# A Jensen-Shannon divergence kernel: row groups in rotating buffers, new column ranges, and a last fold on ScalarE that takes the running sum as its bias

## The chip, the cores and the metric

The kernel runs on one core of a Trainium2 chip. A core has engines that work side by side, each with its own queue of instructions: TensorE (PE, matrix products, with its weight loads shown apart as PEld), VectorE (DVE), ScalarE (ACT), GpSimd (POOL) and SyncE (SP). They share an on-chip memory of 128 partitions (SBUF); TensorE writes to a second one (PSUM). Data comes from the outside memory by DMA, over 16 DMA engines. The metric is the device time of one execution in microseconds.

## The reference

Two inputs of 1,024 rows and 4,096 columns in float32, one float32 result for each row:

```python
m = 0.5 * (p + q)
kl_pm = np.sum(p * np.log(p / (m + 1e-8) + 1e-8), axis=-1)
kl_qm = np.sum(q * np.log(q / (m + 1e-8) + 1e-8), axis=-1)
return (0.5 * (kl_pm + kl_qm)).astype(np.float32)
```

The kernel takes the quotient apart: log p, log q and log m are taken on their own (each with the same scale inside the logarithm, SHIFT), and p(log p - log m) + q(log q - log m) is summed over the columns of a row.

## The kernel before, in words

The rows are dealt to the partitions so that each of 8 row groups (g = 0 to 7) holds 128 rows, one on each partition, with 4,096 columns of p and of q. Within a group the columns are cut into ranges. There are four cuts, each a list of widths for each group: LOADS (what one pair of transfers brings, L20), LOGS (what one logarithm of the data covers, L30), PRODUCTS (how wide a buffer of logarithms is, L40) and SUMS (what one sum p + q covers, L50). A number in what follows counts the ranges of its cut through all groups: q13 is the 14th range of LOGS.

The first two ranges (HW = 2) come in float32, p on SyncE's queue and q on ScalarE's (L171, L172). All others are cast to fp16 under way and are issued by GpSimd (L179, L180), p first, in the order of LOADS, with p and q of a range in the two halves of one tile. Each row group has a tile of its own, so nothing in the loads waits for a buffer.

The operations are named by a letter and a range:

- F (L257): TensorE adds p and q of a SUMS range by two matmuls with the identity into PSUM, 512 columns at a time. There are two PSUM tiles for this, used in turn. For the two float32 ranges VectorE adds them instead (a, L238).
- p and q (L274 to L294): ScalarE's logarithms of the data into a buffer `ab`. For the first SPLIT ranges p and q have an instruction each, later one instruction takes both, with twice the width.
- c (L296): ScalarE's logarithm of the sum, out of PSUM.
- u and x (L309, L318), groups 0 to 5: VectorE subtracts log m from both logarithms, then multiplies by p and q. The product goes over the data in place.
- m and s (L324, L337), groups 6 and 7 (APART = 6): VectorE multiplies p and q by their logarithms, and, apart from that, the sum by its logarithm, which needs no subtraction.
- X, M, S (L348): TensorE adds the columns of a product, 256 at a time, into an accumulator `acc` of the group, with half the identity as weights, or its negative for S.
- The last FUSED_M of the m and FUSED_S of the s are fused: VectorE multiplies and sums along the row in one instruction and keeps a running sum in a column of `run`, so that TensorE has nothing to add.
- f (L374): VectorE folds the 256 columns of `acc` to one number for each row, into a column of `res`. A, in group 7 only (L368): ScalarE does this with a Copy that accumulates; f7 then adds A's number to the running sum.
- W: matmuls whose result is not used.

The order on each engine is written out by hand in three texts: ACT_ORDER (L73), PE_ORDER (L78) and DVE_ORDER (L83). `after` (L405) says what each operation has to wait for: F for its PSUM tile, c for one of 4 buffers (C_BUFS), p and q for one of 5 buffers `ab` (AB_BUFS), products' additions for the accumulator, of which there are two. A loop (L439) emits from each text whatever has all its conditions emitted. Engines keep the order of their texts; the loads of GpSimd are emitted ahead of all that. The end of ScalarE's text is `c30 q29 c31 q30 q31 q32 A7`, of VectorE's `s31 m27 m28 m29 f7`. The result goes out by one DMA of SyncE (L470).

Of the kernel before, what the change touches and what calls it, by code (L numbers as in the profile page):

```python
# [13 lines left out]
AW = 256  # L14
AB_BUFS = 5
C_BUFS = 4

LOADS = [  # L20
    [512, 256, 832, 960, 768, 768],
    [512, 896, 832, 768, 1088],
    [1280, 1408, 1408],
    [1152, 1408, 1536],
    [1280, 1536, 1280],
    [1408, 1408, 1280],
    [256, 1536, 1536, 768],
    [2048, 2048],
]
LOGS = [  # L30
    [512, 256, 832, 960, 768, 768],
    [512, 896, 832, 768, 1088],
    [1280, 1408, 1408],
    [1152, 1408, 1536],
    [1280, 1536, 1280],
    [1408, 1408, 1280],
    [256, 1536, 1536, 768],
    [768, 1024, 896, 512, 512, 384],
]
PRODUCTS = [  # L40
    [512, 256, 832, 1728, 768],
    [512, 896, 832, 1856],
    [1280, 1408, 1408],
    [1152, 1408, 1536],
    [1280, 1536, 1280],
    [1408, 1408, 1280],
    [1792, 1536, 768],
    [768, 1024, 896, 512, 512, 384],
]
SUMS = [  # L50
    [512, 256, 448, 384, 384, 384, 960, 768],
    [512, 896, 832, 768, 1088],
    [1280, 1408, 1408],
    [1152, 1408, 1536],
    [1280, 1536, 1280],
    [1408, 1408, 1280],
    [256, 1536, 1280, 1024],
    [1536, 1408, 1152],
]
HW = 2  # L60
SPLIT = 5

APART = 6
FUSED_M = 1
FUSED_S = 4

# [2 lines left out]


ACT_ORDER = """  # L73
p0 q0 c0 p1 q1 c1 p2 q2 c2 c3 p3 q3 c4 c5 p4 q4 c6 q5 c7 q6 c8 q7 c9 q8 c10 q9 c11 q10 c12
q11 c13 q12 c14 q13 c15 q14 c16 q15 c17 q16 c18 c19 q17 q18 c20 c21 q19 c22 q20 c23 q21
c24 c25 q22 c26 q23 q24 c27 q25 c28 q26 c29 q27 q28 c30 q29 c31 q30 q31 q32 A7
"""
PE_ORDER = """  # L78
W22 F2 F3 X0 X1 F4 F5 X2 X3 F6 X4 X5 F7 F8 X6 F9 X7 F10 X8 F11 X9 F12 X10 X11 F13 W8 X12
F14 F15 X13 F16 X14 F17 X15 F18 X16 F19 X17 F20 X18 F21 X19 F22 X20 F23 X21 F24 F25 X22  # L80
F26 S25 X23 F27 F28 S26 X24 M21 F29 S27 M22 M23 F30 F31 M24 M25 W10 M26 W4 M27 M28
"""
DVE_ORDER = """  # L83
a0 a1 u0 x0 u1 x1 u2 u3 x2 x3 u4 u5 x4 x5 u6 x6 u7 x7 u8 x8 f0 u9 x9 u10 x10 u11 x11 u12
x12 u13 f1 x13 u14 x14 u15 x15 u16 x16 f2 u17 x17 u18 x18 u19 x19 f3 u20 x20 u21 x21 u22
f4 x22 u23 s25 x23 u24 s26 x24 m21 s27 f5 m22 s28 m23 s29 m24 f6 m25 s30 m26 s31 m27 m28
m29 f7
"""


# [1 line left out]
def kernel(  # L92
# [45 lines left out]
        return r[0] >= APART  # L138

    small = ctx.enter_context(tc.tile_pool(name="small", bufs=1))  # L140
    lnp = ctx.enter_context(tc.tile_pool(name="lnp", bufs=AB_BUFS))
    mid = ctx.enter_context(tc.tile_pool(name="mid", bufs=C_BUFS))
    psp = [
# [8 lines left out]
    for i in range(HW):  # L152
        t32 = small.tile([P, 2, loads[i][2]], fp32, tag=f"pq32_{i}")
        early.append(t32)
    data = []
    for g in range(n_rg):
        t16 = small.tile([P, 2, n_cols - (split if g == 0 else 0)], fp16, tag=f"pq{g}")
        data.append(t16)

    def pq(g, c0, w):  # L160
        if g == 0:
            for i in range(HW):
                if loads[i] == (g, c0, w):
                    return early[i]
            c0 -= split
            assert c0 >= 0
        return data[g][:, :, c0 : c0 + w]

    for i in range(HW):
# [3 lines left out]
    warm = small.tile([P, 1], fp32, tag="warm")  # L173
    nc.vector.memset(warm, 1.0)
    nc.scalar.activation(out=warm, in_=warm, func=Act.Ln)  # L175
    def cast_loads(some):
        for g, c0, w in some:
            v = pq(g, c0, w)
            nc.gpsimd.dma_start(out=v[:, 0, :], in_=pv[g, :, c0 : c0 + w])  # L179
            nc.gpsimd.dma_start(out=v[:, 1, :], in_=qv[g, :, c0 : c0 + w])  # L180

    cast_loads(loads[HW : HW + 1])
    ident = small.tile([P, P], fp16, tag="ident")
    make_identity(nc, ident)
    ones = small.tile([P, AW], fp16, tag="ones")
    nc.vector.memset(ones, 1.0)
    zero = small.tile([P, P], fp16, tag="zero")
    nc.vector.memset(zero, 0.0)
    cast_loads(loads[HW + 1 :])
    half = small.tile([P, P], fp16, tag="half")  # L190
    nc.vector.tensor_scalar(
        out=half, in0=ident, scalar1=0.5, scalar2=0.0, op0=Alu.mult, op1=Alu.add
# [22 lines left out]
    for g in range(n_rg):  # L215
        own = [o for o in dve_order if o == ("f", g) or (fused(*o) and range_of(*o)[0] == g)]
        if g < n_rg - 1 or act_folds:
            own = [o for o in own if o[0] != "f"] + [("f", g)]
        chain[g] = own

    ab, c, s, product, acc = {}, {}, {}, {}, {}
# [2 lines left out]
    def next_run(o, g):  # L224
        before = state["last"].get(g, 0.0)
        if o == chain[g][-1]:
            return before, res[:, g : g + 1]
        k = state["used"]
        state["used"] += 1
        state["last"][g] = run[:, k : k + 1]  # L230
        return before, run[:, k : k + 1]
# [92 lines left out]
    def op_m(k):  # L324
        g, c0, w = prods[k]
        u = pq(g, c0, w)
        if not fused("m", k):
            nc.vector.tensor_tensor(out=ab[k], in0=u, in1=ab[k], op=Alu.mult)  # L328
            product["M", k] = ab[k]
            return  # L330
        before, now = next_run(("m", k), g)
        nc.vector.tensor_tensor_reduce(
            out=ab[k], in0=u, in1=ab[k], scale=0.5, scalar=before,
            op0=Alu.mult, op1=Alu.add, accum_out=now,
        )

    def op_s(j):  # L337
        if not fused("s", j):
            nc.vector.tensor_tensor(out=c[j], in0=s[j], in1=c[j], op=Alu.mult)  # L339
            product["S", j] = c[j].unsqueeze(1)  # L340
            return
        before, now = next_run(("s", j), parts[j][0])
        nc.vector.tensor_tensor_reduce(  # L343
            out=c[j], in0=s[j], in1=c[j], scale=-0.5, scalar=before,
            op0=Alu.mult, op1=Alu.add, accum_out=now,
        )

    def add_up(kind, i):  # L348
# [9 lines left out]
        for n, (t, b) in enumerate(todo):  # L358
# [6 lines left out]
                stop=(kind, i) == adds[g][-1] and n == len(todo) - 1,  # L365
            )

    def op_A(g):  # L368
        folded = small.tile([P, 1], fp32, tag="folded")
        unused = small.tile([P, AW], fp16, tag="unused")  # L370
        nc.scalar.activation(out=unused, in_=acc[g][:, :AW], func=Act.Copy, accum_out=folded)  # L371
        state["folded"] = folded

    def op_f(g):  # L374
        if act_folds and g == n_rg - 1:
            nc.vector.tensor_tensor(  # L376
                out=res[:, g : g + 1], in0=state["folded"], in1=state["last"][g], op=Alu.add
            )
            return
        before, now = next_run(("f", g), g)  # L380
        if len(chain[g]) == 1:
            nc.vector.tensor_reduce(out=now, in_=acc[g][:, :AW], axis=AX, op=Alu.add)  # L382
# [22 lines left out]
    def after(kind, i):  # L405
# [19 lines left out]
        if kind == "W":  # L425
            return []
        if kind == "f":
            if act_folds and i == n_rg - 1:
                return chain[i][:-1] + [("A", i)]
            return chain[i][: chain[i].index(("f", i))] + adds[i]  # L430
        if kind == "A":
            return adds[i]
        return []

    accumulator(0)
    ops = dict(a=op_a, F=op_F, p=op_p, q=op_q, c=op_c, u=op_u, x=op_x, m=op_m, s=op_s, f=op_f, A=op_A)
    queues = [list(pe_order), list(act_order), list(dve_order)]
    emitted = set()
    while any(queues):  # L439
        moved = False  # L440
# [21 lines left out]
    want |= {(k.upper(), i) for k, i in want if k in "xms" and not fused(k, i)}  # L462
    want |= {("f", g) for g in range(n_rg)} | {("p", i) for i in range(SPLIT)}
    if act_folds:
        want.add(("A", n_rg - 1))
    assert emitted == want
    pe_order = [o for o in pe_order if o[0] != "W"]
    assert len(pe_order) + len(act_order) + len(dve_order) == len(want)

# [31 lines left out]
```

## Time and profile before

| | us |
|---|---|
| median of 4 runs (lowest to highest) | 97.81 (97.71 to 98.01) |
| profiled execution | 98.02 |
| its span, first to last instruction | 96.3 |
| ScalarE busy | 89.7 |
| VectorE busy | 81.7 |
| TensorE matmuls busy | 69.9 |
| ScalarE idle before logs of the data, in all | 1.6 |
| first logarithm of data starts, last one ends | 4.21, 92.50 |
| result in its tile | 93.90 |

The mean granted TensorE clock is 0.994. Lines of the profile name the engine, the line of the kernel, the operation, what is written and read, and the shapes (partitions x elements, type). In a timeline the first two columns are start and duration in us; what stands in brackets is how long the engine was idle just before and what ended that. Where neighbours of one kind are merged (x2), the shape is that of the first. In lines of groups the numbers after the bar are the busy time in us, the mean of one instruction in ns, and the idle time before them.

### The profile page before, as it was taken

What the parts mean: (1) busy time and instruction counts of PE and PEld (TensorE: products, weight loads), DVE (VectorE), ACT (ScalarE), POOL (GpSimd) and SP (SyncE); (2) the same over time, 40 slices, a digit from 0 to 9 for tenths busy, and PEclk for the clock granted to TensorE, in tenths of its full rate; (3) what the DMA queues carried; (4) which work ended last, traced back from release to release, by engine and by line L of the source; (5) the groups of instructions that cost most, each with busy time, mean ns of one, the idle gap of its engine ahead of it and who ended that gap; (6) DMA issues with size and microseconds to landing.
All of it is one profiled execution on the core that took longest, in us unless ns stands there. A gap on an engine that the chain in (4) does not pass through costs nothing.

```text
span 96.3 us, 1311 instructions
## 1 busy us (share of the span) xinstructions
PE 69.9 (73%) x468; PEld 44.7 (46%) x468; DVE 81.7 (85%) x87; ACT 89.7 (93%) x74; POOL 29.3 (30%) x60
## 2 busy tenths in 40 slices
PE   0797884976598568696785974984977979797740
PEld 0573441644456144462452642652652766566520
DVE  1279869999964988998979989979999999999990
ACT  3599999999979999999999999999999999999960
POOL 5974466443242424242332423336400000000000
PEclk9999999999999999999999999999999999999997
DMA  1999999999999999999999999999999999400000
GB/s 40 331 179 196 204 205 209 207 211 215 208 214 210 209 212 214 213 210 213 211 213 210 211 212 211 208 211 208 217 202 216 220 211 215 90 0 3 0 0 2
DMA packets 8503, 17.25 MB, mean 179 GB/s; under 512 B 1073, under 2 KB 3889, under 8 KB 8497
## 3 DMA queue, kind: packets, MB, share of 16 engines
q0 software_dynamic: 7776, 16.39, 89.9%
q1 hardware_dynamic: 432, 0.40, 1.4%
q10 hardware_dynamic: 288, 0.39, 1.2%
q8 instruction: 3, 0.05, 0.2%
q14 instruction: 4, 0.02, 0.1%
HBM read 33.55 MB, written 0.00 MB: 349 GB/s over the span
## 4 chain that ended last, share of the span: by engine, by line
ACT 48%; issue 22%; DVE 6%; PE 1%; ACTq 0%; DVEq 0%
ACT ab_t L281 30%; ACT c_t L299 18%; DVE t L321 2%; DVE c_t L343 1%; DVE ab_t L311 1%; PE acc_t L360 1%; DVE ab_t L328 1%; ACT unused L371 0%; ACTq L299 0%; DVE res L376 0%; ACTq L496 0%; ACTq L281 0%; DVEq L321 0%; DVE run L343 0%
## 5 line engine op out<-in xcount | busy, mean ns | idle before, releaser
L281 ACT ACTIVATE ab_t<-t 128x2816 f16<-128x2816 f16 (+15 forms) x38 | 62.6, 1685 | 1.6 <-DMA t<-in_p_dram 1.1
L265 PE MATMUL st<-t,ident 128*128 128x512 f16 (+4 forms) x144 | 34.0, 350 | 9.0 <-DMA t<-in_q_dram 7.9
L311 DVE TENSOR_TENSOR ab_t<-ab_t,c_t 128x2816 f16<-128x2816 f16 (+12 forms) x25 | 29.3, 1180 | 6.9 <-ACT c_t L299 6.1
L360 PEld LDWEIGHTS <-half 128*128 128x128 f16 x268 | 25.2, 97 | 20.1 <-issue 15.8
L299 ACT ACTIVATE c_t<-st 128x1408 f16<-128x1408 f32 (+13 forms) x30 | 32.3, 1099 | 0.0
L360 PE MATMUL acc_t<-t,half 128*128 128x256 f16 (+2 forms) x200 | 23.9, 264 | 8.2 <-DVE t L321 7.9
L321 DVE TENSOR_TENSOR t<-t,ab_t 128x2816 f16<-128x2816 f16 (+11 forms) x23 | 28.2, 1234 | 1.2
L265 PEld LDWEIGHTS <-ident 128*128 128x128 f16 x144 | 13.4, 97 | 23.1 <-issue 13.1
L179 POOL DMA_DIRECT2D t<-in_p_dram x27 | 14.5, 537 | 20.3 <-DMA t<-in_p_dram 19.3
L180 POOL DMA_DIRECT2D t<-in_q_dram x27 | 14.4, 532 | 19.7 <-DMA t<-in_q_dram 19.7
L360 PE MATMUL acc_t<-ab_t,half 128*128 128x256 f16 x68 | 8.9, 270 | 3.1 <-DVE ab_t L328 2.8
L328 DVE TENSOR_TENSOR ab_t<-t,ab_t 128x1536 f16<-128x1536 f16 (+5 forms) x8 | 9.3, 1171 | 0.1
L253 PE MATMUL acc_t<-ones,ident 128*128 128x256 f16 x22 | 4.2, 377 | 3.1 <-POOL ident masks.py:199 3.1
L253 PEld LDWEIGHTS <-ident 128*128 128x128 f16 x22 | 2.9, 136 | 4.1 <-POOL ident masks.py:199 3.1
L339 DVE TENSOR_TENSOR c_t<-st,c_t 128x256 f16<-128x256 f32 (+2 forms) x3 | 3.6, 1216 | 0.0
L343 DVE CUSTOM_DVE_ANT_0 c_t<-st,c_t,run 128x1408 f16<-128x1408 f32 (+1 forms) x2 | 3.1, 1546 | 0.0
L343 DVE CUSTOM_DVE_ANT_0 c_t<-st,c_t 128x1024 f16<-128x1024 f32 (+1 forms) x2 | 3.0, 1484 | 0.0
L253 PE MATMUL acc_t<-ones,zero 128*128 128x256 f16 x22 | 2.9, 273 | 0.0
L175 ACT ACT_TABLE_LOAD x1 | 1.3, 1283 | 1.7 <-PEq L485 1.7
L382 DVE TENSOR_REDUCE res<-acc_t 128x1 f32<-128x256 f32 x6 | 2.5, 417 | 0.0
L253 PEld LDWEIGHTS <-zero 128*128 128x128 f16 x22 | 2.1, 98 | 0.2
L321 DVE TENSOR_TENSOR ab_t<-t,ab_t 128x1024 f16<-128x1024 f32 (+1 forms) x2 | 1.9, 958 | 0.1
(24 smaller groups left out, 9.7 us busy)
## 6 DMA issues: line engine op xcount, KB each, us to landing
t<-in_p_dram POOLq DMA_DIRECT2D x5, 352.0 KB, 12.6
t<-in_q_dram POOLq DMA_DIRECT2D x5, 352.0 KB, 13.0
t<-in_p_dram POOLq DMA_DIRECT2D x4, 384.0 KB, 11.8
t<-in_q_dram POOLq DMA_DIRECT2D x4, 384.0 KB, 12.0
t<-in_p_dram POOLq DMA_DIRECT2D x4, 320.0 KB, 13.1
t<-in_q_dram POOLq DMA_DIRECT2D x4, 320.0 KB, 12.8
t<-in_p_dram POOLq DMA_DIRECT2D x2, 512.0 KB, 13.1
t<-in_q_dram POOLq DMA_DIRECT2D x2, 512.0 KB, 14.4
```

What stands on the lines that cost most here:

```text
L179: nc.gpsimd.dma_start(out=v[:, 0, :], in_=pv[g, :, c0 : c0 + w])
L180: nc.gpsimd.dma_start(out=v[:, 1, :], in_=qv[g, :, c0 : c0 + w])
L253: nc.tensor.matmul(out=acc[g][:, :AW], lhsT=weights, rhs=ones, start=alone, stop=alone)
L265: nc.tensor.matmul(out=st[:, b : b + m], lhsT=ident, rhs=v[:, t, b : b + m], start=t == 0, stop=t == 1,)
L281: nc.scalar.activation(out=ab[k][:, which, o : o + w], in_=pq(g, c0, w)[:, which, :], func=Act.Ln, bias=TINY, scale=SHIFT,)
L299: nc.scalar.activation(out=c_t[:, :w], in_=s[j], func=Act.Ln, bias=SHIFT * 1e-8, scale=SHIFT * 0.5)
L311: nc.vector.tensor_tensor(out=v, in0=v, in1=c[j].unsqueeze(1).to_broadcast([P, 2, parts[j][2]]), op=Alu.subtract,)
L321: nc.vector.tensor_tensor(out=into, in0=u, in1=v, op=Alu.mult)
L328: nc.vector.tensor_tensor(out=ab[k], in0=u, in1=ab[k], op=Alu.mult)
L339: nc.vector.tensor_tensor(out=c[j], in0=s[j], in1=c[j], op=Alu.mult)
L343: nc.vector.tensor_tensor_reduce(out=c[j], in0=s[j], in1=c[j], scale=-0.5, scalar=before, op0=Alu.mult, op1=Alu.add, accum_out=now,)
L360: nc.tensor.matmul(out=acc[g][:, :m], lhsT=less if kind == "S" else half, rhs=v[:, t, b : b + m], start=(kind, i) == adds[g][0] and n == 0 ...
```

## The change

Row groups no longer have a tile each: six tiles (DATA_BUFS) rotate, so that groups 6 and 7 take those of groups 0 and 1. A load is an operation L of its own with an order of its own; a load of group g waits until all products of group g - 6 have been added by TensorE.

All four cuts have new widths. The number of ranges: LOADS 29 before and 28 after, LOGS 33 and 28, PRODUCTS 30 and 24, SUMS 32 and 31. The widest buffer of logarithms grows from 1,856 to 2,816 columns; in groups 3 and 4 one logarithm of data covers 2,048 columns and so two loads. In groups 0 and 1 the first 7 ranges have p and q apart (SPLIT 5 to 7). The last group's logarithms end in ranges of 256, 256 and 128 columns, where they ended in 512, 512 and 384. The fused sums are the last five (FUSED_S 4 to 5), so that one of group 6 is among them. The three orders are new.

In group 7 there is no f any more. A is an Identity of ScalarE with the running sum as its bias, which adds it to each of the 256 columns before they are accumulated; so that it counts once, the fused operations of group 7 scale their sums by 1/256. A writes the result's column itself. f6 comes last on VectorE.

```diff
+DATA_BUFS = 6
 LOADS = [
-    [512, 256, 832, 960, 768, 768],
-    [512, 896, 832, 768, 1088],
-    [1280, 1408, 1408],
+    [352, 608, 864, 1088, 1184],
+    [1280, 1536, 1280],
     [1152, 1408, 1536],
-    [1280, 1536, 1280],
-    [1408, 1408, 1280],
-    [256, 1536, 1536, 768],
+    [1024, 1024, 1024, 1024],
+    [1024, 1024, 1024, 1024],
+    [1664, 1152, 1280],
+    [1920, 896, 640, 640],
     [2048, 2048],
 ]
 LOGS = [
...
+    [352, 608, 864, 1088, 1184],
+    [1280, 1536, 1280],
     [1152, 1408, 1536],
-    [1280, 1536, 1280],
+    [2048, 2048],
+    [2048, 2048],
     [1408, 1408, 1280],
-    [256, 1536, 1536, 768],
-    [768, 1024, 896, 512, 512, 384],
+    [1280, 1280, 1536],
+    [1152, 1024, 768, 512, 256, 256, 128],
 ]
 PRODUCTS = [
...
+    [352, 608, 864, 2272],
+    [1280, 2816],
+    [2560, 1536],
+    [2048, 2048],
+    [2048, 2048],
+    [1408, 2688],
+    [1280, 1280, 1536],
+    [1152, 1024, 768, 512, 256, 256, 128],
 ]
 SUMS = [
...
+    [352, 608, 512, 352, 896, 736, 640],
+    [1280, 1536, 1280],
     [1152, 1408, 1536],
-    [1280, 1536, 1280],
+    [1024, 1024, 1024, 1024],
+    [1024, 1024, 1024, 1024],
     [1408, 1408, 1280],
-    [256, 1536, 1280, 1024],
-    [1536, 1408, 1152],
+    [1280, 1280, 1536],
+    [1536, 1408, 640, 512],
 ]
-SPLIT = 5
+SPLIT = 7
-FUSED_S = 4
+FUSED_S = 5
 ACT_ORDER = """
...
+p0 q0 c0 p1 q1 c1 p2 q2 c2 c3 p3 q3 c4 p4 q4 c5 c6 p5 q5 c7 p6 q6 c8 q7 c9 q8 c10 q9 c11
+q10 c12 c13 q11 c14 c15 q12 c16 c17 q13 c18 c19 q14 c20 q15 c21 c22 q16 c23 q17 c24 q18
+c25 q19 c26 q20 c27 q21 c28 q22 c29 q23 c30 q24 q25 q26 q27 A7
 """
 PE_ORDER = """
...
+W22 F2 F3 X1 X0 F4 X2 X3 F5 F6 X4 F7 X5 X6 F8 X7 F9 F10 X8 F11 X9 X10 F12 F13 X11 F14 W8
+F15 X12 F16 X13 F17 X14 F18 X15 F19 X16 F20 X17 X18 F21 F22 X19 X20 F23 X21 F24 X22 F25
+S24 F26 X23 M14 F27 M15 S25 W6 F28 M16 F29 M17 F30 W4 M18 W4 M19 W3 M20 M21 M22
 """
 DVE_ORDER = """
...
+a0 u0 a1 x0 u1 x1 u2 u3 x2 x3 u4 x4 u5 u6 x5 x6 u7 f0 x7 u8 x8 u9 x9 u10 x10 f1 u11 x11
+u12 x12 u13 u14 x13 x14 f2 u15 u16 x15 x16 u17 u18 x17 x18 f3 u19 u20 x19 x20 u21 f4 x21
+u22 x22 u23 s24 x23 m14 s25 m15 s26 f5 m16 s27 m17 s28 m18 s29 m19 s30 m20 m21 m22 m23 f6
 """
...
+    datap = ctx.enter_context(tc.tile_pool(name="datap", bufs=DATA_BUFS))
...
-    cast_loads(loads[HW : HW + 1])
+    def op_L(i):
+        g, c0, w = loads[i]
+        if g not in data:
+            t16 = datap.tile([P, 2, n_cols], fp16, tag="pq")
+            data[g] = t16
+        v = pq(g, c0, w)
+        nc.gpsimd.dma_start(out=v[:, 0, :], in_=pv[g, :, c0 : c0 + w])
+        nc.gpsimd.dma_start(out=v[:, 1, :], in_=qv[g, :, c0 : c0 + w])
+    op_L(HW)
...
-            out=ab[k], in0=u, in1=ab[k], scale=0.5, scalar=before,
+            out=ab[k], in0=u, in1=ab[k], scale=0.5 * share(g), scalar=before,
...
-            out=c[j], in0=s[j], in1=c[j], scale=-0.5, scalar=before,
+            out=c[j], in0=s[j], in1=c[j], scale=-0.5 * share(g), scalar=before,
...
+    def share(g):
+        return 1.0 / AW if act_folds and g == n_rg - 1 else 1.0
     def op_A(g):
-        folded = small.tile([P, 1], fp32, tag="folded")
         unused = small.tile([P, AW], fp16, tag="unused")
-        nc.scalar.activation(out=unused, in_=acc[g][:, :AW], func=Act.Copy, accum_out=folded)
-        state["folded"] = folded
+        before, now = next_run(("A", g), g)
+        nc.scalar.activation(
+            out=unused, in_=acc[g][:, :AW], func=Act.Identity, bias=before, accum_out=now
+        )
     def op_f(g):
-        if act_folds and g == n_rg - 1:
-            nc.vector.tensor_tensor(
-                out=res[:, g : g + 1], in0=state["folded"], in1=state["last"][g], op=Alu.add
-            )
-            return
...
         if kind == "A":
-            return adds[i]
+            return chain[i][:-1] + adds[i]
+        if kind == "L":
+            g = loads[i][0] - DATA_BUFS
+            return adds[g] if g >= 0 else []
         return []
...
+    load_order = [("L", i) for i in range(HW + 1, len(loads))]
+    queues = [load_order, list(pe_order), list(act_order), list(dve_order)]
```

## The prediction

> **What bounds the kernel now.** I read the page's busy shares first, then ScalarE's timeline, then GpSimd's (it issues the casting loads), then the last stretch of all engines. The time is made against the profiled execution: 98.02 us, span 96.3 us, so 1.72 us lie around the span; the median of the runs is 97.81, 0.21 lower. A change in the span is taken over to the median as it stands.
>
> From the page:
> ```profile
> PE 69.9 (73%) x468; PEld 44.7 (46%) x468; DVE 81.7 (85%) x87; ACT 89.7 (93%) x74; POOL 29.3 (30%) x60
> DMA  1999999999999999999999999999999999400000
> ```
> ScalarE and the DMA engines both have no room: the transfers are dense until slice 34 (about 82.9 us), ScalarE to the end. From ScalarE's timeline:
> ```profile
> 24.19 2.08 ACT L281 ACTIVATE ab_t<-t 128x2176 f16<-128x2176 f16 x1
> 26.10 1.14 ACT L299 ACTIVATE c_t<-st 128x1088 f16<-128x1088 f32 x1
> 27.77 2.34 ACT L281 ACTIVATE ab_t<-t 128x2560 f16<-128x2560 f16 x1 [0.53 <-DMA t<-in_q_dram]
> 30.02 1.22 ACT L299 ACTIVATE c_t<-st 128x1280 f16<-128x1280 f32 x1
> 31.14 2.55 ACT L281 ACTIVATE ab_t<-t 128x2816 f16<-128x2816 f16 x1
> ...
> 34.82 2.54 ACT L281 ACTIVATE ab_t<-t 128x2816 f16<-128x2816 f16 x1
> 37.26 1.33 ACT L299 ACTIVATE c_t<-st 128x1408 f16<-128x1408 f32 x1
> 38.49 2.12 ACT L281 ACTIVATE ab_t<-t 128x2304 f16<-128x2304 f16 x1
> ```
> and from GpSimd's:
> ```profile
> 22.86 0.53 POOL L179 DMA_DIRECT2D t<-in_p_dram  x1 [0.78 <-DMA t<-in_p_dram]
> 24.16 0.53 POOL L180 DMA_DIRECT2D t<-in_q_dram  x1 [0.77 <-DMA t<-in_q_dram]
> 26.38 0.53 POOL L179 DMA_DIRECT2D t<-in_p_dram  x1 [1.70 <-DMA t<-in_p_dram]
> 27.97 0.53 POOL L180 DMA_DIRECT2D t<-in_q_dram  x1 [1.06 <-DMA t<-in_q_dram]
> 29.64 0.53 POOL L179 DMA_DIRECT2D t<-in_p_dram  x1 [1.14 <-DMA t<-in_p_dram]
> 31.34 0.53 POOL L180 DMA_DIRECT2D t<-in_q_dram  x1 [1.18 <-DMA t<-in_q_dram]
> ```
> Eight casting transfers go out without a wait at the start; after that each issue waits for a landing. So I take issue n+8 as the sign that transfer n landed, about 0.23 us earlier (the matmul that waited for q started at 9.99, GpSimd's issue stands at 10.23). Transfer 20, the first q of row group 2, so landed at 27.74, and ScalarE started its log at 27.77: it ran hand to mouth. The next landed at 31.11; its log began at 31.14. The one at 34.55 (issue 34.79) was used at 34.82. After that ScalarE is late by itself and never waits. The law: q of a range lands at 7.6 us (the matmul wait at 7.62) plus 512 bytes (one column of one input, 128 rows of 4 bytes) at 420 GB/s (twice the 210 written, since the cast halves the bytes), 1.219 ns, for each column of p and of q after the first 3,200. It puts the end of group 1 at 23.67 (23.93 seen) and the end of group 2 at 33.66 (34.55 seen). The 0.65 us more came in one jump, at the 1.70 us wait, while the page's GB/s row there reads 208 to 214: one lane was late, not the whole flow.
>
> **What the Trainium skill says.** "DMA: Bandwidth & Descriptors", section "Why a DMA increments its semaphore by 16 and not by 1": a transfer counts as landed only when each of its engines has reported, so one late engine holds it. The trace agrees with the jump at full rate, but shows no single engine. "ScalarE: Activation LUTs", "What ACT_TABLE_LOAD costs": 0.833 ns an element, and about 93 ns for each pointer operand. The step from 31.14 to 33.60 for 2,816 elements is 2.46 us, 0.11 over the elements; and the same 256 elements from PSUM take 463 ns with a bias and 383 without:
> ```profile
> L299 ACT ACTIVATE c_t<-st 128x256 f16<-128x256 f32 x1 | 0.5, 463 | 0.0
> L371 ACT ACTIVATE unused<-acc_t 128x256 f16<-128x256 f32 x1 | 0.4, 383 | 0.7 <-PE acc_t L360 0.7
> ```
> The same page, "Table sets: the hidden batching unit": identity and copy sit in every set as filler, so Identity in place of Copy should load no table. No run here shows Identity.
>
> **Part by part.**
> *ScalarE's sum.* Steps in the trace: a log of SBUF data costs its elements at 0.8333 ns plus 0.095 us (2.44 for 2,816 at 34.82), a log of the sums in PSUM plus 0.052 (1.23 for 1,408 at 37.26). Before: from 34.82, 65,664 elements, 20 and 17 instructions: 54.72+1.90+0.88 = 57.50, that is 92.32; the last log ends at 92.50, so 0.18 for an end. The change keeps 98,304 elements and has 66 instructions for 70 (35 logs of loads for 38, 31 of sums for 32): 0.34 us less in all. But that is worth only what the landings let through. In the new order, latest landing plus remaining work plus 0.18:
> - q2 (1,824 columns in): lands 8.2, 83.16 left: 91.5. q4: 13.7+77.64+0.18 = 91.5. q7: 23.9+67.78+0.18 = 91.9.
> - q9 (10,752 columns): 30.8+61.41+0.18 = 92.4.
> - q10 (end of group 2): 34.55 as before, 66,048 elements, 18 and 19 instructions left = 57.74: 92.47.
> - q11, now 2,048 columns, needs two loads of 1,024, 14,336 columns in. Between the landings 37.33 and 40.78 (issues 37.56 and 41.01) of 13,440 and 14,848 columns that is 39.5; 52.85 left: 92.53.
> - q12: 44.45+47.53+0.18 = 92.2; later ones less.
> So ScalarE ends its last log at about E = 92.5, as before: a first load of 352 columns may start it near 3.9 instead of 4.21 (160 columns of both inputs, 0.39 us), and it waits that off again. From start to end without waits it would be 3.9+86.94+0.18 = 91.0, the lower bound.
>
> *The loads' buffers.* A load of group 6 waits for the products of group 0 to be added, which the fold of group 0 at 19.83 shows done; GpSimd gets to transfer 41 at about 49.6 by the old issues. Group 7 waits for group 1 (fold at 32.68), issues near 60. Queued behind such a wait is every later load, but the margin is over 25 us: cost 0. That wait is absent from the old trace; a satisfied one costs at most some tens of ns on a queue that waits 39 us for landings anyway.
>
> *Sums just in time.* c24 needs 1,920 columns landed: 64.5 (end of group 5, issue 64.74) plus 3,840 x 1.219 = 69.2, plus six matmuls, 1.1 us (1.02 for five seen): 70.3, where ScalarE wants it at 92.5-0.18-21.79 = 70.5. c27: 79.4+1.6 = 81.0 against 81.2. c28: 83.0+1.2 = 84.2 against 84.5. All hold, by 0.2 to 0.3; if a wide load lands 0.5 later they cost 0.3.
>
> *VectorE.* 24 pairs of subtraction and product for 25, one product more in groups 6 and 7; the elements are the same except 192 more columns in fp32 at the start, 0.2 us in the addition and 0.2 in the product, hidden by its 6.9 us of waiting before subtractions. In the end it must follow ScalarE. An operation takes its elements at 0.96 GHz (two at once in fp16) plus 0.075 between starts (3,584: 1.94 us). From the end of c28: s28 ends at 1.57, m18 (log ready at 1.80) 2.97, s29 3.71, m19 4.67, s30 5.28, m20 5.89, m21 6.23, m22 6.60, while ScalarE's last log ends at 6.54. It follows with 0.06 lost. Fusing one sum more changes a product into one of the same rate and spares PE its adds.
>
> *The end.* Now:
> ```profile
> 92.53 1.02 DVE L332 CUSTOM_DVE_ANT_0 ab_t<-t,ab_t,run 128x768 f16<-128x768 f16 x1
> 93.23 0.38 ACT L371 ACTIVATE unused<-acc_t 128x256 f16<-128x256 f32 x1 [0.73 <-PE acc_t L360]
> 93.48 0.08 DVE L332 DVE_READ_ACCUMULATOR2_ANT run<- 128x1 f32 x1
> 93.51 0.19 ACT L371 ACTIVATION_READ_ACCUMULATOR unused<-acc_t 128x1 f32 x1
> 93.74 0.16 DVE L376 TENSOR_TENSOR res<-folded,run 128x1 f32<-128x1 f32 x1 [0.18 <-ACT unused L371]
> ```
> From the last log's end (92.50) to the result (93.90) 1.40 us. New: m23 has 256 elements, 1,017-512/0.96 = 484 ns; with its read it ends at E+0.06+0.50 = E+0.56. A7 now waits for it: 0.04 handover (93.70 to 93.74 the other way), 0.47 from its start to the end of its read (93.23 to 93.70) and 0.08 for the bias: E+1.15. M22 is two matmuls behind m22, done at about E+0.45, so not last. f6 beside it: 0.47+0.08 after m23, earlier than A7. The addition, 0.16 and its handover, is gone. Gain 0.25 (0.15 if the handover doubles, 0.31 if VectorE loses nothing). The output's transfer stays as it is.
>
> Sum: E unchanged (92.50 to 92.53), the end 0.25 shorter: 97.81-0.25 = 97.56; with E at q10's 92.47, 97.5. I take 97.5.
>
> **Rivals.**
> 1. *The late lane does not come back* (other widths, other moments). Then group 2 ends near 33.7, q10 gives 91.6 and c24 comes in time too: 0.85 us less, with the end 1.1: 96.7. For it: the delay was one jump. Against: all later landings keep 0.8 to 1.0 behind the law, and the new loads of group 1 are as wide as those at which it came. Chance 0.22.
> 2. *Slower: q11 waits for its second load.* A further delay like the first, 0.65 us, before the end of its two loads: 40.15+52.85+0.18 = 93.2, result 94.3, 0.45 later: 98.3. It decides from a landing at 39.7 (E of 92.75). For it: this log has no slack and needs four transfers in place of two. Against: only one such jump in 54 transfers. Chance 0.14.
> 3. *Identity brings a table load*, 1.28 us as the one at the start, 0.5 of it beside m23: 98.4. Chance 0.04.
> 4. *The end gains nothing*, because VectorE lags or the read-accumulator hand-over is longer: 97.8. Chance 0.1.
>
> **How the numbers follow.** The first forecast has 0.5. A difference of 0.2% (0.2 us) is about what a measurement can tell from none. Forecast: 0.36 of its half clearly faster, 0.12 within, 0.02 slower; rival 1 faster; rivals 2 and 3 slower; rival 4 within: faster 0.36+0.22 = 0.58, same 0.12+0.10 = 0.22, slower 0.02+0.14+0.04 = 0.20. The range takes rival 1 and reaches to where rival 2 begins to cost: 96.6 to 98.2; the forecast's own is 97.2 to 97.8.
>
> **What would show it.** ScalarE's logs of groups 0 to 3 should start within 0.1 us of landings, and after q11 none should wait; its last log should end at 92.3 to 92.7. The result should stand 1.1 to 1.2 us after it, with A7 near 0.46 us and no second table load. A last log before 92 means the lane was not late; a wait before q11, c24 or c27 means that these bind.

## The result, and the profile after

The changed kernel takes 97.76 us (median of 36 runs), the kernel before, run beside it, 97.94 us (55 runs): ratio 0.9982, 95% interval 0.997 to 0.9995, so 0.05 to 0.29 us less. That is faster, but by less than was predicted: 97.5 was 0.31 below the 97.81 it started from; what was measured is 0.18. The span of the profiled execution fell from 96.3 to 96.0 us. Ratios here and below leave out executions more than 1.5% above the fastest of their kernel; medians count all.

ScalarE's timeline of the changed kernel, at the place where the loads used to bind and at the end:

```profile
28.66 1.11 ACT L300 ACTIVATE c_t<-st 128x1152 f16<-128x1152 f32 x1
30.08 2.55 ACT L282 ACTIVATE ab_t<-t 128x2816 f16<-128x2816 f16 x1 [0.31 <-DMA t<-in_q_dram]
32.54 1.32 ACT L300 ACTIVATE c_t<-st 128x1408 f16<-128x1408 f32 x1
33.76 2.75 ACT L282 ACTIVATE ab_t<-t 128x3072 f16<-128x3072 f16 x1
...
81.82 2.23 ACT L282 ACTIVATE ab_t<-t 128x2304 f16<-128x2304 f16 x1
84.55 1.34 ACT L300 ACTIVATE c_t<-st 128x1408 f16<-128x1408 f32 x1 [0.50 <-PE st L266]
85.79 1.90 ACT L282 ACTIVATE ab_t<-t 128x2048 f16<-128x2048 f16 x1
...
90.02 2.40 ACT L282 ACTIVATE ab_t<-t 128x1024 f16<-128x1024 f16 x4
93.09 0.47 ACT L377 ACTIVATE unused<-acc_t,run 128x256 f16<-128x256 f32 x1 [0.66 <-PE acc_t L362]
93.46 0.19 ACT L377 ACTIVATION_READ_ACCUMULATOR unused<-acc_t,run 128x1 f32 x1
```

The log at 30.08 is q9, still hand to mouth with its load; q10, at 33.76, follows its predecessor without a wait, 0.8 us before the moment at which the prediction let its data land. So ScalarE was early. Then, at 84.55, c28 waits 0.50 us for its sum on TensorE, a wait that the kernel before does not have. The last log ends at 92.42 (90.02+2.40), before at 92.50. The result stands at 93.65, before at 93.90.

What c28 waited for is in TensorE's timeline of the same kernel:

```profile
81.61 0.82 PE L254 MATMUL acc_t<-ones,zero 128*128 128x256 f16 x6
82.27 0.81 PE L266 MATMUL st<-t,ident 128*128 128x512 f16 x3
83.81 0.70 PE L266 MATMUL st<-t,ident 128*128 128x512 f16 x3 [0.74 <-DMA t<-in_q_dram]
```

F28 has six matmuls. It did three, then stood until q of the last load landed, at about 83.8, and ended at 84.51. The sum covers columns 1,536 to 2,944 of group 7; the last load brings columns 2,048 to 4,096. F28 needs 896 of its 2,048 columns and waits for all of them.

To see where the landings went, I read GpSimd's issues as the prediction did and took off the prediction's law. Positive is late; each number is for q of the last range that ends at or before the column count:

| columns of each input | before | changed |
|---|---|---|
| end of the second casting load (2,560; 2,912) | +0.06 | -0.56 |
| 8,192 | +0.26 | -0.55 |
| 9,472; 9,344 | +0.95 | +0.13 |
| 12,288 | +0.90 | +0.06 |
| 20,480 | +0.98 | +0.39 |
| 26,368; 26,496 | +0.92 | +0.27 |

The changed kernel starts 0.6 us ahead, and meets a jump at the same place (0.68 against 0.69 us; that the two sizes agree is chance, they run from 0.28 to 1.04 in the twelve traces of this document).

### The profile page after: what moved, and what is told of

Its sections match the earlier page's. It is cut to its first block, busy times and chain, and to the rows that moved or that the text cites. A ratio compares the mean times of both kernels' runs of the same rounds, so it can differ in the third digit from the quotient of the medians.

```text
span 96.0 us, 1291 instructions
## 1 busy us (share of the span) xinstructions
PE 69.4 (72%) x461; PEld 44.6 (46%) x461; DVE 80.9 (84%) x86; ACT 89.8 (94%) x70; POOL 28.3 (29%) x58
## 4 chain that ended last, share of the span: by engine, by line
DMA 81%; issue 7%; DVE 3%; ACT 3%; POOL 2%; PE 1%; DVEq 0%; ACTq 0%; POOLq 0%
DMA t<-in_p_dram 68%; DMA t<-in_q_dram 13%; ACT ab_t L282 2%; DVE c_t L345 2%; DVE ab_t L329 1%; POOL t L180 1%; PE st L266 1%; POOL t L181 1%; ACT unused L377 0%; DVEq L500 0%; POOL ident masks.py:199 0%; POOL ident masks.py:197 0%; ACTq L500 0%; ACT c_t L300 0%; POOLq L500 0%
## 5 line engine op out<-in xcount | busy, mean ns | idle before, releaser
L282 ACT ACTIVATE ab_t<-t 128x2560 f16<-128x2560 f16 (+15 forms) x35 | 61.2, 1782 | 1.0 <-DMA t<-in_p_dram 0.7
L312 DVE TENSOR_TENSOR ab_t<-ab_t,c_t 128x2048 f16<-128x2048 f16 (+10 forms) x24 | 28.9, 1223 | 8.1 <-ACT c_t L300 5.4
L300 ACT ACTIVATE c_t<-st 128x1024 f16<-128x1024 f32 (+9 forms) x29 | 31.1, 1101 | 0.5 <-PE st L266 0.5
L362 PE MATMUL acc_t<-t,half 128*128 128x256 f16 (+1 forms) x192 | 23.5, 268 | 9.2 <-DVE t L322 9.0
L322 DVE TENSOR_TENSOR t<-t,ab_t 128x2048 f16<-128x2048 f16 (+9 forms) x22 | 27.5, 1272 | 0.5
L362 PE MATMUL acc_t<-ab_t,half 128*128 128x256 f16 (+2 forms) x74 | 9.0, 267 | 1.3 <-DVE ab_t L322 0.7
L329 DVE TENSOR_TENSOR ab_t<-t,ab_t 128x2560 f16<-128x2560 f16 (+6 forms) x9 | 9.6, 1088 | 0.3 <-ACT ab_t L282 0.2
L345 DVE CUSTOM_DVE_ANT_0 c_t<-st,c_t,run 128x1408 f16<-128x1408 f32 (+2 forms) x3 | 3.3, 1102 | 0.5 <-ACT c_t L300 0.5
L345 DVE CUSTOM_DVE_ANT_0 c_t<-st,c_t 128x1536 f16<-128x1536 f32 x2 | 3.5, 1752 | 0.0
L340 DVE TENSOR_TENSOR c_t<-st,c_t 128x1280 f16<-128x1280 f32 x2 | 3.0, 1486 | 0.0
```

Of the source, the lines that this page charges most:

```text
L282: nc.scalar.activation(out=ab[k][:, which, o : o + w], in_=pq(g, c0, w)[:, which, :], func=Act.Ln, bias=TINY, scale=SHIFT,)
L300: nc.scalar.activation(out=c_t[:, :w], in_=s[j], func=Act.Ln, bias=SHIFT * 1e-8, scale=SHIFT * 0.5)
L312: nc.vector.tensor_tensor(out=v, in0=v, in1=c[j].unsqueeze(1).to_broadcast([P, 2, parts[j][2]]), op=Alu.subtract,)
L322: nc.vector.tensor_tensor(out=into, in0=u, in1=v, op=Alu.mult)
L345: nc.vector.tensor_tensor_reduce(out=c[j], in0=s[j], in1=c[j], scale=-0.5 * share(g), scalar=before, op0=Alu.mult, op1=Alu.add, accum_out=now,
L362: nc.tensor.matmul(out=acc[g][:, :m], lhsT=less if kind == "S" else half, rhs=v[:, t, b : b + m], start=(kind, i) == adds[g][0] and n == 0 ...
```

## The experiments

Every ratio is to the kernel before, run beside it on the same chip. The changed kernel's own is 0.9982 (0.997 to 0.9995).

**The last load, cut in two.** The theory: c28 pays for the last load's width. One line:

```diff
     [1920, 896, 640, 640],
-    [2048, 2048],
+    [2048, 896, 1152],
 ]
 LOGS = [
```

> The changed kernel with the last load of group 7 (2,048 columns) cut into 896 and 1,152; all logs, sums and orders as they are. Theory (the last transfer holds c28): c28 waited 0.50 us in the changed kernel because its sum reaches into the last 2,048 columns, whose q landed at about 83.8; with the cut those columns are there some 2.8 us earlier, the wait goes, the last log ends near 91.9 instead of 92.42, and the time falls by 0.4 to 0.5 us (ratio to before about 0.994). Rival (TensorE's order or its PSUM tile holds the sum): no wait goes, ratio 0.998 as now. Second rival (two transfers more land later in all): slower than now, 0.999 to 1.002.

Measured: 97.17 us, ratio 0.9878 (0.9842 to 0.9914). TensorE and ScalarE, in the timelines of this kernel:

```profile
82.36 1.35 PE L266 MATMUL st<-t,ident 128*128 128x512 f16 x6
```

```profile
81.63 2.23 ACT L282 ACTIVATE ab_t<-t 128x2304 f16<-128x2304 f16 x1
83.75 1.34 ACT L300 ACTIVATE c_t<-st 128x1408 f16<-128x1408 f32 x1
...
89.22 2.40 ACT L282 ACTIVATE ab_t<-t 128x1024 f16<-128x1024 f16 x4
```

F28 runs through its six matmuls at once, c28 follows q21 without a wait, and the last log ends at 91.62. The wait was the transfer's: TensorE's order and its PSUM tile are as they were. In this trace the landings were also about 0.2 us earlier than in the changed kernel's, so its 0.8 us is more than the 0.5 of the wait. The ratio is below the 0.994 expected, and it rests on six executions, so I ran it again:

> last_load_cut once more on this chip, for the next one to be compared with, and since it rests on few executions. Theory: c28 does not wait, last log near 91.7; 0.5 to 0.8 us faster than the changed kernel, ratio to before 0.990 to 0.994. Rival (its 0.988 was a matter of that chip's runs of before): 0.996 to 0.998.

Measured: 97.21 us, ratio 0.9905 (0.9873 to 0.9936), again clear of the changed kernel's interval. This version beats both kernels, the changed one by 0.8 to 1.0%. In its trace, too, c28 has no wait, though its landings after the jump were about 0.4 us later than the changed kernel's (+0.53 at 9,344 columns); so its last log ends at 92.22 and not near the 91.7 expected. The two ratios make the gain over the changed kernel 0.75 to 1.0 us. The wait that went accounts for 0.26 to 0.50 (the size of c28's wait in two traces with the uncut load); where the rest comes from is not shown.

The same cut in the kernel before is the control, since nothing waits there:

```diff
     [256, 1536, 1536, 768],
-    [2048, 2048],
+    [2048, 896, 1152],
 ]
 LOGS = [
```

> The kernel before with its last load of 2,048 columns cut into 896 and 1,152 as in last_load_cut. Theory (only a sum that reaches into the last load and is wanted before it lands gains, and none waits in the kernel before): ratio 0.999 to 1.001. Rival (smaller last loads make all of the last landings earlier, or the program a good deal faster by themselves): 0.990 to 0.996, as last_load_cut's 0.988.

Measured: ratio 0.9987 (0.9969 to 1.0005). The cut by itself brings nothing that can be told from none. It frees a wait where there is one.

**Do the six tiles hold the loads?** The trace of the changed kernel could be read so. GpSimd's timeline before the first loads of groups 6 and 7:

```profile
53.42 0.53 POOL L180 DMA_DIRECT2D t<-in_p_dram  x1 [1.37 <-PE st L266]
...
66.76 0.53 POOL L180 DMA_DIRECT2D t<-in_p_dram  x1 [2.02 <-ACT ab_t L282]
```

These are the two issues that gained a wait for a buffer, and the profile names TensorE and ScalarE as releasers. A tile for each group takes the waits away:

```diff
-DATA_BUFS = 6
+DATA_BUFS = 8
-    datap = ctx.enter_context(tc.tile_pool(name="datap", bufs=DATA_BUFS))
+    datap = ctx.enter_context(tc.tile_pool(name="datap", bufs=DATA_BUFS - 1))
     data = {}
+    first_tile = small.tile([P, 2, n_cols - split], fp16, tag="pq_first")
+    data[0] = first_tile
-            assert c0 >= split
+            c0 -= split
+            assert c0 >= 0
```

> The changed kernel with a tile for each row group again, so that no load waits for a buffer. The trace of the changed kernel names TensorE and ScalarE as what ended two waits of GpSimd before the first loads of groups 6 and 7 (1.37 and 2.02 us). Theory (these waits are really for earlier transfers, eight at a time, and the buffers had long been free): nothing moves, ratio within 0.1% of the changed kernel's 0.998, c28 still waits. Rival (the buffers hold the loads): the loads of groups 6 and 7 go out 0.15 to 0.8 us earlier, c28's wait of 0.50 shrinks or goes, ratio 0.993 to 0.996.

Measured: ratio 1.0005 (0.9974 to 1.0036). GpSimd's timeline of this kernel:

```profile
53.28 0.53 POOL L183 DMA_DIRECT2D t<-in_p_dram  x1 [1.11 <-DMA t<-in_p_dram]
...
66.33 0.53 POOL L183 DMA_DIRECT2D t<-in_p_dram  x1 [1.74 <-DMA t<-in_p_dram]
```

The same two issues wait 1.11 and 1.74 us, at nearly the same moments, and now an earlier transfer is named. That the buffers had long been free is also in the changed kernel's own trace: VectorE folds group 0 at 20.55 and group 1 at 32.53, each after all its products have been added, and the issues come at 53.42 and 66.76. The name says only which of the engines waited for had signalled last.

The ratio alone would not decide. In this trace 2.82 us pass between the result and the last instruction, where every other trace of this document has 2.33 to 2.35, so half a microsecond of its time lies behind the result and has nothing to do with the loads. One sign for the rival remains: with six tiles the first issue of group 7 waits 2.00 to 2.02 us in all seven traces, here 1.74. But the issue behind it comes at 68.63, no earlier than in most of them (68.59 to 68.95), and c28 still waits, 0.26 us, for the same transfer (its F28 stands until 83.68). So the six tiles may cost one issue some 0.3 us; no later issue or landing shows it.

**The new fold alone, in both directions.** First the changed kernel with the old fold (Copy on ScalarE, addition on VectorE, sums of group 7 unscaled):

```diff
-        before, now = next_run(("A", g), g)
-        nc.scalar.activation(
-            out=unused, in_=acc[g][:, :AW], func=Act.Identity, bias=before, accum_out=now
-        )
+        nc.scalar.activation(out=unused, in_=acc[g][:, :AW], func=Act.Copy, accum_out=folded)
+        state["folded"] = folded
...
-        return 1.0 / AW if act_folds and g == n_rg - 1 else 1.0
+        return 1.0
...
-u22 x22 u23 s24 x23 m14 s25 m15 s26 f5 m16 s27 m17 s28 m18 s29 m19 s30 m20 m21 m22 m23 f6
+u22 x22 u23 s24 x23 m14 s25 m15 s26 f5 m16 s27 m17 s28 m18 s29 m19 s30 m20 m21 m22 m23 f6 f7
```

> The changed kernel with the fold of group 7 as before: a Copy that accumulates on ScalarE, then the addition on VectorE, fused sums unscaled. Theory (the gain at the end comes from the short last range, the new fold gives next to nothing): the Copy starts when TensorE's last addition ends (93.02), its read ends at 93.5, the addition at 93.71; 0.06 us later than the changed kernel's 93.65, ratio to before 0.9985 to 0.9995. Rival (the fold is the gain, as the prediction's sum for the end reads): 0.25 us later, ratio about 1.0005.

Measured: ratio 0.9971 (0.9949 to 0.9993), not to be told from the changed kernel. Its end:

```profile
92.34 0.48 DVE L332 CUSTOM_DVE_ANT_0 ab_t<-t,ab_t,run 128x256 f16<-128x256 f16 x1
92.89 0.38 ACT L376 ACTIVATE unused<-acc_t 128x256 f16<-128x256 f32 x1 [0.63 <-PE acc_t L361]
93.40 0.16 DVE L381 TENSOR_TENSOR res<-folded,run 128x1 f32<-128x1 f32 x1 [0.17 <-ACT unused L376]
```

The last log ends at 92.26 and the result stands at 93.56, 1.30 us later, where the changed kernel has 1.23 and the kernel before 1.40. This distance repeats: it is 1.23 in all seven traces with the new fold and the short last range, and 1.40 in all three with neither. So with the short range in place the fold is worth 0.07 us of the 0.17, and the short range the other 0.10; the rival's 1.0005 is outside the interval.

Then the kernel before with the new fold, its last range left at 384 columns:

```diff
-        nc.scalar.activation(out=unused, in_=acc[g][:, :AW], func=Act.Copy, accum_out=folded)
-        state["folded"] = folded
+        before, now = next_run(("A", g), g)
+        nc.scalar.activation(
+            out=unused, in_=acc[g][:, :AW], func=Act.Identity, bias=before, accum_out=now
+        )
...
-m29 f7
+m29
```

> The kernel before with only the new fold: Identity with the running sum as bias, the addition gone. Theory: ScalarE now waits for the fused product of the last 768 elements, whose read ends at 93.56, in place of TensorE's 93.21; 0.04 and 0.55 us more give 94.15, 0.25 later than 93.90: ratio about 1.0025. Rival (the addition and its hand-over are saved whatever the ranges): 0.16 to 0.2 us earlier, ratio 0.998.

Measured: ratio 1.0008 (0.9986 to 1.003). Its timeline at the end:

```profile
92.08 1.02 DVE L333 CUSTOM_DVE_ANT_0 ab_t<-t,ab_t,run 128x768 f16<-128x768 f16 x1
93.03 0.08 DVE L333 DVE_READ_ACCUMULATOR2_ANT run<- 128x1 f32 x1
93.20 0.47 ACT L377 ACTIVATE unused<-acc_t,run 128x256 f16<-128x256 f32 x1 [1.16 <-DVE run L333]
93.58 0.19 ACT L377 ACTIVATION_READ_ACCUMULATOR unused<-acc_t,run 128x1 f32 x1
```

The fold now hangs on the long fused product. The last log ends at 92.05, the result stands 1.72 us later: the end is 0.32 longer than the kernel before's. The expected 1.0025 lies in the ratio's interval, the rival's 0.998 does not; 0.32 us would be 1.0033, just beyond it, and why the times show less than the trace is open. (The profiled execution, at 97.87 us the fastest of its 22, was not longer than that of before because its landings were 0.46 us earlier with the same loads, +0.44 for +0.90 at 12,288 columns.) Alone, then, the new fold lengthens the end; with a last range of 256 elements it shortens it a little.

**Where the early landings come from.** The changed kernel brings 960 columns in float32 on the queues of SyncE and ScalarE, the kernel before 768. I gave the kernel before 960:

```diff
 LOADS = [
-    [512, 256, 832, 960, 768, 768],
+    [512, 448, 832, 768, 768, 768],
...
 SUMS = [
-    [512, 256, 448, 384, 384, 384, 960, 768],
+    [512, 448, 448, 384, 384, 384, 768, 768],
```

(LOGS as LOADS, PRODUCTS 512, 448, 832, 1536, 768.)

> The kernel before with the second float32 load of 448 columns in place of 256 (and its logs, products and sums with it; the fourth load, of 960, becomes 768), so that 960 columns come in float32 as in the changed kernel. Theory (the changed kernel's casting transfers land 0.55 us ahead of the old law because the first two loads, on queues of their own, carry more): the landings of groups 0 to 2 move 0.4 to 0.6 us earlier against columns brought, ScalarE's first waits shrink, its last log ends 0.3 to 0.5 us earlier, ratio to before 0.995 to 0.997. Rival (the wide casting loads or the narrow first range make them land earlier): nothing moves, ratio 1.000, or slower by VectorE's 0.4 us more of float32 work.

Measured: 97.72 us, ratio 0.996 (0.9942 to 0.9979). Against the law its landings stand at -0.57 (2,560 columns), -0.36 (8,192) and +0.30 (12,288). The last log ends at 91.89. So these columns alone give the lead at the start (-0.57 for -0.56), and two thirds of it at 8,192 columns, without the wider casting loads and the narrow first range. The page's GB/s rows of the kernel before and the changed kernel:

```profile
GB/s 40 331 179 196 204 205 209 207 211 215 208 214 210 209 212 214 213 210 213 211 213 210 211 212 211 208 211 208 217 202 216 220 211 215 90 0 3 0 0 2
```

```profile
GB/s 46 378 206 209 214 209 212 213 208 212 213 210 208 210 211 208 210 210 208 211 209 216 210 209 210 214 221 201 205 206 224 220 207 210 58 0 0 0 0 2
```

A slice is 2.4 us. Most of what the first two show more is only that a float32 column is written with twice the bytes: 192 columns of p and of q are 0.10 of the 0.13 MB. Slices 3 to 5 run fuller, 206, 209 and 214 for 179, 196 and 204; that is 0.12 MB, 0.6 us of casting transfers at 210 GB/s, and everything after is earlier by about that. The lead is not there in every execution: of the eight traces of the changed kernel and its variants seven have -0.41 to -0.78 at 8,192 columns, and one (cut_fewer_idle, below) has +0.10; why is open.

**More of it, with the cut.** I moved 256 more columns into the second float32 load, with the last load cut as above:

```diff
-    [352, 608, 864, 1088, 1184],
+    [352, 864, 608, 1088, 1184],
...
-    [352, 608, 512, 352, 896, 736, 640],
+    [352, 864, 256, 352, 896, 736, 640],
```

(LOGS as LOADS, PRODUCTS 352, 864, 608, 2272.)

> last_load_cut with 864 columns in the second float32 load and 608 in the first casting one (they were 608 and 864), and logs, products and sums with them. Theory (float32 loads of the start put all landings ahead): landings another 0.4 to 0.6 us earlier, the wait of q9 (0.18 to 0.31) goes, last log 0.1 to 0.3 earlier than in last_cut_again, ratio 0.001 to 0.003 lower. Rival (the second load now lands too late for p1, and VectorE's float32 work of 0.5 us more holds ScalarE back): as last_cut_again or up to 0.4 us slower.

Measured: 100.26 us (median of all 11 executions), ratio 1.0099 (1.0055 to 1.0144): a miss, on the rival's side and beyond it. The landings did come earlier, -0.70 against -0.50, but TensorE's and ScalarE's timelines show what it cost:

```profile
11.38 1.22 PE L362 MATMUL acc_t<-ab_t,half 128*128 128x256 f16 x12 [3.44 <-DVE ab_t L322]
12.44 0.92 PE L266 MATMUL st<-t,ident 128*128 128x512 f16 x4
```

```profile
13.46 0.92 ACT L300 ACTIVATE c_t<-st 128x896 f16<-128x896 f32 x1 [1.41 <-PE st L266]
```

The wider second load landed later, as the rival said: p1 starts at 5.69 after a wait of 0.83 for it (5.07 and 0.19 in the changed kernel). VectorE's float32 product of the second range then took 1.96 us (1.42 in the changed kernel) and started at 9.36 (7.84); TensorE stood 3.44 us at its addition (X1), with F4 queued behind it, and c4 waited 1.41 us for F4. The last log ends at 93.22, 1.6 us after the cut kernel's. The profiled execution is near the fastest of this kernel's runs (98.44 to 103.24). The longer ones were granted a lower mean TensorE clock: 1.0 in the two of 98.4 to 98.6 us, 0.977 to 0.983 in five of 99.3 to 100.5, 0.916 to 0.948 in four of 100.8 to 103.2. Why this kernel is granted less is open.

**What makes the landings jump.** Every trace up to here has the jump between 8,192 and 9,472 columns, in kernels with different ranges. The page lists a queue that is not the kernel's:

```profile
q8 instruction: 3, 0.05, 0.2%
```

If these three packets are what holds the data, and if TensorE, with by far the most instructions, asks for them, then the jump should follow its count. The changed kernel with 2 for 22 idle matmuls at the start has 40 instructions fewer in front:

```diff
-W22 F2 F3 X1 X0 F4 X2 X3 F5 F6 X4 F7 X5 X6 F8 X7 F9 F10 X8 F11 X9 X10 F12 F13 X11 F14 W8
+W2 F2 F3 X1 X0 F4 X2 X3 F5 F6 X4 F7 X5 X6 F8 X7 F9 F10 X8 F11 X9 X10 F12 F13 X11 F14 W8
```

> The changed kernel with 2 in place of 22 idle matmuls at the start of TensorE's order, so that each later instruction of TensorE is 40 places (20 matmuls, 20 weight loads) earlier in its stream. In all traces so far the landings fall behind by 0.4 to 1.0 us in one jump between 8,192 and 9,472 columns of each input (24 to 26.5 us), and by up to 0.25 again near 53 us. Theory A (one DMA engine is held for the fetch of TensorE's next block of instructions, which the profile lists as 3 packets of 17 KB each): the jump follows TensorE's count of instructions and comes about 3 to 5 us later, between 9,344 and 12,288 columns, and the third one, near 79 us, falls behind the last landing or moves too. Theory B (it belongs to the moment or to the place in the data): the jump stays between 8,192 and 9,344 columns. For the time: equal to the changed kernel's 0.998 within 0.003, unless TensorE now starts at a lower clock, which would delay F2 and cost up to 0.5 us.

GpSimd's timeline of the changed kernel, then of this one:

```profile
23.35 0.53 POOL L181 DMA_DIRECT2D t<-in_q_dram  x1 [1.08 <-DMA t<-in_q_dram]
25.92 0.53 POOL L180 DMA_DIRECT2D t<-in_p_dram  x1 [2.04 <-DMA t<-in_p_dram]
```

```profile
29.33 0.53 POOL L181 DMA_DIRECT2D t<-in_q_dram  x1 [1.23 <-DMA t<-in_q_dram]
32.23 0.53 POOL L180 DMA_DIRECT2D t<-in_p_dram  x1 [2.37 <-DMA t<-in_p_dram]
```

The long wait moved from 25.92 to 32.23: the landings are at -0.81 of the law at 10,752 columns and at +0.20 at 12,288. The ratio is 0.9984 (0.996 to 1.0008), as the changed kernel. What the later jump gave went elsewhere: TensorE's first matmuls ran slower without the idle ones (F4's four took 1.69 us for 0.92, at a granted clock of 1.0 in both), and c4 waited 1.26 us. The profiled execution, 98.42 us, is one of those with a lower mean clock (see below). The cut kernel with the same edit:

> last_load_cut with 2 in place of 22 idle matmuls at the start. Theory A (instruction fetch): as in fewer_idle_matmuls, the jump moves to between 9,344 and 12,288 columns; theory B: it stays. For the time: ratio to before 0.988 to 0.993 as the cut alone, since ScalarE is ahead of TensorE's first sums by little: if they come later for a cold clock, up to 0.5 us worse.

Measured: ratio 0.9971 (0.9948 to 0.9994), a miss for the 0.988 to 0.993; the jump is between 10,752 and 12,288 columns there too (+0.07 to +0.35). Two waits for TensorE stand in its trace: c4's 0.61 us, and

```profile
27.73 1.24 ACT L300 ACTIVATE c_t<-st 128x1280 f16<-128x1280 f32 x1 [1.05 <-PE st L266]
```

The second belongs to this execution (98.86 us): its granted clock is 0.50 from 24.0 to 27.2 us. It can't stand for the kernel. But the eleven executions with a mean clock of 0.995 or more took 97.5 to 97.95 us, mean 97.75, and those of the cut kernel at that clock (on other chips) about 97.2; so some 0.6 us of the cut's gain are lost at full clock too, of the size of c4's wait.

The idle matmuls go with the clock as well. In 11 of 22 executions of each of the two kernels without them the mean granted clock was 0.982 or lower; of the kernel before, run beside them, in 9 of 43, and of the changed kernel in 3 of 36. It is not the idle matmuls alone, since cut_more_fp32 has all 22 and a clock of 0.983 or lower in 9 of 11; the cause is open. At 97 us, 0.982 is what one stretch of 3.4 us at half clock gives.

Do the packets hold the data? The packed trace keeps the start, the length and the size of every packet. The three of q8 have 16,384 bytes each and take 0.89 to 1.05 us, where a data packet of 4,096 bytes takes 0.32. Their times, and how many instructions TensorE (weight loads counted) had started by then, as far as the trace records them:

| | ten traces with 22 idle matmuls | 2 idle, uncut | 2 idle, cut |
|---|---|---|---|
| first packet, us | 22.9 to 24.1 | 29.16 | 30.00 |
| TensorE's instructions by then | 179 to 207 | 203 | 209 |
| second packet, us | 47.9 to 52.3 | 55.49 | 56.60 |
| TensorE's instructions by then | 451 to 455 | 457 | 463 |

The first packet comes just ahead of the first late landing in each of the twelve, and it moved with it. While one of the 36 packets is under way, the others move 4 to 8% fewer bytes per us than in the 3 us before, with 5.5% as the median; one engine of the 16 is 6.3%. So the jump follows TensorE's instruction count, and the packet takes about one engine's worth of the data flow while it lasts. What stays open: which engine it is, why the jump is 0.28 us in one trace and 1.04 in another with packets of the same length, and why the second packet is followed by at most a small or passing delay. (A second instruction queue, q14, has up to three packets of 8,192 bytes in the span, of 0.32 to 0.40 us; no jump follows them.)

## Why the prediction was wrong

The forecast's gain, 0.31 us, was 0.25 from the end and 0.03 from the last log's end at 92.47; the rest is 97.53 rounded to 97.5. (Its own list has a later bound, q11's 92.53.) The measured 0.18 (0.05 to 0.29) agrees with the end alone, which the traces put at 0.17; how much the last log's end adds can't be told, since it stands at 92.42, 92.26 and 92.29 in three traces with the changed kernel's loads (its own, old_fold, own_tiles), and at 92.50, 92.67 and 92.05 in three with those of the kernel before (its own, before_last_cut, before_new_fold).

**The end** was the mis-sized term and the step that failed: 1.40 to 1.15 predicted, 1.40 to 1.23 in the traces, 0.17 us for 0.25. VectorE's timeline of the changed kernel, beside ScalarE's lines above:

```profile
92.51 0.48 DVE L333 CUSTOM_DVE_ANT_0 ab_t<-t,ab_t,run 128x256 f16<-128x256 f16 x1
92.91 0.08 DVE L333 DVE_READ_ACCUMULATOR2_ANT run<- 128x1 f32 x1
92.91 0.48 DVE L387 CUSTOM_DVE_ANT_0 junk<-acc_t,ones,run 128x256 f16<-128x256 f32 x1
```

m23 ends with its read at 92.99, 0.57 after the last log (0.56 predicted). A7 takes 0.56 from its start to the end of its read (0.55 predicted), 0.473 us for the Identity against the Copy's 0.383: the bias costs 0.09, as "ScalarE: Activation LUTs" has it ("What ACT_TABLE_LOAD costs"), and no second table load appears, as its section on table sets led me to expect.

What was wrong is the step between: "0.04 handover (93.70 to 93.74 the other way)". From VectorE's read to ScalarE's start it is 0.10 here, and 0.09 in the kernel before with the new fold (93.11 to 93.20), where VectorE is named and TensorE was done by 92.75. Here the profile names TensorE: its last addition, put at E+0.45, came at 93.02, E+0.60, level with m23. From TensorE's last addition to a Copy that waits for it alone it is 0.03 (93.20 to 93.23 in the kernel before; ends of matmuls are modelled), so TensorE by itself would have let A7 start at 93.05. A handover of 0.04 would therefore have won 0.04 us, not 0.06: two waits end almost together here, and the forecast had one of them too short and the other too early.

**The last log's end**, 92.5 predicted and 92.42 found, is right for a wrong reason. Two steps fail and cancel:

- "q10 (end of group 2): 34.55 as before" and q11's 39.5. The law was anchored at the kernel before's third load, and I priced the wider float32 loads only as an earlier start that ScalarE "waits off again". They moved the landings 0.6 us forward, as before_more_fp32 shows. q10 was bound by nothing at 33.76; q9's wait at 30.08, plus its 61.41 left and 0.18, gives 91.7.
- "c28. 83.0+1.2 = 84.2 against 84.5". I took the end of the dense DMA slices for the landing of the last load. That row is a mean over 16 engines and does not say when the last one ends: in the kernel before's trace the last data packet ends at 84.03. The law itself puts the landing at 83.6, and in the changed kernel it came at 83.8. And the early ScalarE asked for the sum at 84.05, not at 84.5. That cost 0.50, as last_load_cut shows by its absence. The rest of the way from 91.7 to 92.42, 0.25 us, is ScalarE's steps being longer than the two prices, spread over 60 us.

A slip on which nothing rests: the way from start to end without waits, by the prediction's own prices, is 86.86 us and not 86.94.

**Right:** that landings and not instruction counts set ScalarE's end; no cost of the rotating tiles that reaches the landings (own_tiles); VectorE following with 0.06 lost (m23 starts 0.09 after the last log); c24 and c27 just in time, no wait at either. Rival 1 was half right: the late lane did come back, as large as before, but on landings that were early; its 0.85 us stood at 34 us and was mostly gone by 85. Rivals 2 to 4 did not occur: no log of two loads waited, there was no table load, and the end did gain.

So the change moved much and gained little because most of what it wins at the start, it hands back at the last load. One line of the load list returns it.

## What to carry to other kernels

When two limits are near each other, write the latest-landing sum for every range to the last one and keep it for the new schedule: an engine that comes early asks for the last data early too. A sum or a log waits for the whole of the transfer that holds its last column, so the last transfers want to be cut where their first user ends. A releaser named by the profile on an instruction with several waits is not taken on trust: take one of the waits away, and look up when the named work had really ended. A ratio is read together with where in the trace the time lies, and at which granted clock the execution ran.

## What the runs showed that I had not expected

- A jump of 0.3 to 1.0 us in the landings that follows TensorE's place in its instruction stream: 40 instructions fewer in front moved it from 25 to 32 us, and the 16,384-byte packet on the instruction queue with it. While it is under way the data flow is lower by about one engine's share. "DMA: Bandwidth & Descriptors" ("Why a DMA increments its semaphore by 16 and not by 1") fits how one held engine delays a whole transfer; no trace here names the engine.
- The same loads stood at +0.44 and at +0.90 us of the law in two profiled executions, and at -0.50 and +0.10 from the start on in two others (the cut kernel with and without the idle matmuls). A sum made against one profile carries that.
- 192 columns more of float32 in the second load move the later landings 0.6 us forward (ratio 0.996), in the kernel before; 256 more again, on top of the cut in the changed kernel, move them another 0.2 us up to the jump and lose 2% (0.9905 to 1.0099), where the trace shows a later second load and a wait on VectorE's float32 product.
- The idle matmuls at the start pay: without 20 of them F4 takes 1.69 us for 0.92, and half of the executions, for one in five of the kernel before beside them, were granted a mean clock of 0.982 or lower.
